# A hybrid attention layer on one core: 40 narrow columns of the input projection go with the second block

## The chip, the core and the metric

The kernel runs on one core of one Trainium2 chip. The metric is the device time of one execution in microseconds (us), as the median over several executions. The matrix engine is called TensorE or PE, and its weight loads PEld; VectorE is DVE, ScalarE is ACT, GpSimd is POOL, SyncE is SP. SP issues nearly all loads.

## The reference

One decoder layer for 256 rows of width 2048, all in float32. What matters here is the combined input projection: one product with `w_in` (2048 x 5672), whose columns feed both groups of heads.

```python
GLA_HEADS, GLA_GATE_RANK, NSA_HEADS = 4, 16, 8
PROJ_SIZES = (GLA_QKV, GLA_GATE_RANK, GLA_VW, NSA_QW, NSA_KVW, NSA_KVW, NSA_KVW, NSA_KVW, NSA_KVW, NSA_KVW, 3 * NSA_HEADS)

n = rms_norm(x, attn_norm_g)
proj = n @ w_in
offsets = np.cumsum(PROJ_SIZES)[:-1].tolist()
(g_qkv, g_lr, g_out, nq, kc, vc, ks, vs, kw, vw, ng) = jnp.split(proj, offsets, axis=-1)
...
log_a = jax.nn.log_sigmoid((gate_lr @ gate_w2 + gate_b).astype(jnp.float32)) / GLA_GATE_TAU
o = rms_norm(o, norm_g) * jax.nn.silu(out_gate.astype(jnp.float32)).reshape(b_, s, h, GLA_DV)
...
gates = jax.nn.sigmoid(gate_logits.astype(jnp.float32)).reshape(b_, s, hk, g, 3).transpose(0, 2, 3, 1, 4)
return gb[..., 0:1] * o_cmp + gb[..., 1:2] * o_sel + gb[..., 2:3] * o_win
...
h = x + jnp.concatenate([gla_out, nsa_out], axis=-1) @ w_out
m = rms_norm(h, ffn_norm_g)
return h + (jax.nn.silu(m @ w_gate) * (m @ w_up)) @ w_down
```

Two pieces of the projection are narrow: `g_lr`, the 16 low rank columns that make the decay of the linear attention, and `ng`, the 24 columns that gate the three branches of the sparse attention. The other columns come in 11 pieces of 512: the output gate (2), q and k and v of the linear attention (4), the compressed, selected and window keys with their values (3), and the sparse queries (2).

## The kernel before, in words

**Blocks, chunks, steps.** The projection runs as 11 blocks (`proj`, L297), driven in a fixed order by the `drive` calls at L1376 to L1388. The order is: both halves of the output gate, four blocks for the linear attention, the compressed block (`C_KC`), the selected block (`C_KS`), the window-key block (`C_KW`), two query blocks. A block has four chunks of 512 rows of `w_in`; in the texts chunks are counted through from 0, so that block 2 has chunks 4 to 7 and the window-key block 32 to 35. For each chunk the weights are loaded by one DMA of 1 MB from SP (`load`, L135), into one of three buffers `raw`. `split` (L138) cuts them into two float32r parts, two of the four row tiles at a time: ScalarE copies `raw` to `hi` (L144), VectorE subtracts and writes `lo` (L145). `chunk` (L278) then issues 24 products (L289) for each piece of at most 512 columns: four row tiles `k`, two halves `t` of the 256 rows, three products each (hi by hi, hi by lo, lo by hi). I call one (k, t) with its three products a step; so a chunk has 8 steps.

**Narrow columns.** A bank of the accumulator memory holds 512 columns. Block 1 loads 16 + 512 columns from `C_LR` on, as the low rank columns lie directly ahead of the output gate; so it works in two pieces of 256 and 272 columns and issues two products where a 512-wide block issues one. In the same way the window-key block loads 512 + 24 columns, in pieces of 256 and 280. At its end, `ev_go(0)` (L384) scales the 16 columns and puts `gla_gate` (L438) on the list `later`, and `ev_kv(1)` (L706) makes the sigmoid of the 24.

**The first block** has loads of its own (L184 to L192), cut finer, and takes its weights from `first_chunk` (L353), in turn with the transposes of `x` (L213).

**Side work.** `drive` (L105) lets the block's products yield units; for so many units `side` takes one step of a task from `urgent` or `later`: transposes, the decay passes of the linear attention (L565 to L572 on VectorE, for two heads and seven levels), its score products (L598 on TensorE), key normalisation (L735 to L753 on VectorE). A third list, `background`, is stepped by a counter: `sum_rows` (L1089) loads a pair of row tiles of the feed-forward weights `w_gate` and `w_up` (1 MB in two loads from SP, L1096), adds them on VectorE (L1101, four adds) and writes the sums back from GpSimd's queue (L1105).

**Order.** Each engine runs its own queue in order. A scheduler settles the order from the program's order and from the `issue_after` hints (`behind`). So a `lo` on VectorE can stand behind an add that waits for its load, and a load on SP behind one that waits for a buffer.

## Time and profile before

| | |
|---|---|
| median of three runs | 1101.02 us (1100.81 to 1101.49) |
| span of the profiled execution | 1099.1 us |
| around the span | 1.9 us |
| TensorE busy | 1094.3 us, 100% |
| VectorE busy | 996.3 us, 91% |
| ScalarE busy | 744.5 us, 68% |
| first block begins (TensorE) | 6.1 us |
| first product with `lo` in block 2 | 34.1 us |
| first product with `lo` in the window-key block | 200.8 us |
| one 512-wide chunk without side work | 5.44 us |

How to read it: a timeline row has the start in us, the time that it spans, engine, line, operation, output and inputs, how often it ran in a row (x2), and in brackets the idle time ahead of it and what ended it. Products overlap on TensorE, so the distance between their starts counts and not the duration. A row of groups ends with busy time, the mean of one in ns and the idle time before. In the queue rows of the DMA view stand packets, MB and the time that the packets took, as a share of 16 engines over the window.

### The profile page before, as it was taken

What the parts mean: (1) busy time and instruction counts of PE and PEld (TensorE: products, weight loads), DVE (VectorE), ACT (ScalarE), POOL (GpSimd) and SP (SyncE); (2) the same over time, 40 slices, a digit from 0 to 9 for tenths busy, and PEclk for the clock granted to TensorE, in tenths of its full rate; (3) what the DMA queues carried; (4) which work ended last, traced back from release to release, by engine and by line L of the source; (5) the groups of instructions that cost most, each with busy time, mean ns of one, the idle gap of its engine ahead of it and who ended that gap; (6) DMA issues with size and microseconds to landing.
All of it is one profiled execution on the core that took longest, in us unless ns stands there. A gap on an engine that the chain in (4) does not pass through costs nothing.

```text
span 1099.1 us, 14686 instructions
## 1 busy us (share of the span) xinstructions
PE 1094.3 (100%) x5294; PEld 900.8 (82%) x5294; DVE 996.3 (91%) x1289; ACT 744.5 (68%) x1014; POOL 81.1 (7%) x150
## 2 busy tenths in 40 slices
PE   9999999999999999999999999999999999999998
PEld 8888888987777887888888888888888888888887
DVE  6578879987799988997999999999999999999998
ACT  7645567555675587667585867768585877768685
POOL 4110001033100100000000000000000000000000
PEclk9999999999999999999999999999999999999999
DMA  7999978468886946785566657576665768677663
GB/s 271 340 338 369 394 259 284 167 243 290 307 280 246 331 159 244 234 317 190 182 230 209 211 197 253 184 248 209 213 230 202 251 214 294 208 259 232 235 231 115
DMA packets 128818, 271.15 MB, mean 247 GB/s; under 512 B 7093, under 2 KB 9177, under 8 KB 128746
## 3 DMA queue, kind: packets, MB, share of 16 engines
q1 hardware_dynamic: 115466, 223.61, 59.2%
q0 software_dynamic: 12672, 46.14, 11.3%
q8 instruction: 41, 0.67, 0.2%
q10 hardware_dynamic: 608, 0.47, 0.1%
q14 instruction: 31, 0.25, 0.1%
HBM read 247.12 MB, written 23.07 MB: 246 GB/s over the span
## 4 chain that ended last, share of the span: by engine, by line
PE 89%; DVE 3%; DMA 3%; issue 2%; ACT 2%; POOL 0%; SPq 0%; DVEq 0%; ACTq 0%; POOLq 0%
PE bank L289 41%; PE bank L1169 39%; PE bank L213 3%; DMA g<-in_w_up_dram 2%; PE bank L1310 2%; DVE lo L145 2%; PE bank L967 1%; PE bank L893 1%; DMA raw<-in_w_out_dram 1%; DVE g L1101 1%; ACT hi L144 1%; PE bank L598 0%; PE bank L800 0%; PE bank L203 0%; ACT g L559 0%
## 5 line engine op out<-in xcount | busy, mean ns | idle before, releaser
L1169 PE MATMUL bank<-ftwo,g 128*128 128x512 f32 x1842 | 430.7, 393 | 0.2 <-ACT ftwo L656 0.2
L1169 PEld LDWEIGHTS bank<-ftwo,g 128*128 128x128 f32 x1842 | 341.2, 188 | 77.0 <-DVE ftwo L657 4.0
L289 PE MATMUL bank<-hi,g 128*128 128x512 f32 (+1 forms) x1088 | 322.7, 377 | 0.0
L657 DVE TENSOR_TENSOR ftwo<-fraw,ftwo 128x1536 fp32r<-128x1536 f32 (+1 forms) x130 | 256.8, 1976 | 7.7 <-ACT ftwo L656 6.6
L656 ACT ACTIVATE ftwo<-fraw 128x1536 fp32r<-128x1536 f32 (+1 forms) x130 | 216.0, 1663 | 28.9 <-DMA fraw<-in_w_up_dram 19.1
L289 PE MATMUL bank<-ftwo,g 128*128 128x512 f32 x960 | 220.7, 390 | 0.0
L289 PEld LDWEIGHTS bank<-hi,g 128*128 128x128 f32 x1088 | 191.9, 189 | 30.3 <-issue 1.0
L289 PEld LDWEIGHTS bank<-ftwo,g 128*128 128x128 f32 x960 | 179.7, 188 | 38.3 <-ACT bank L1281 0.3
L144 ACT ACTIVATE hi<-raw 128x1024 fp32r<-128x1024 f32 (+3 forms) x124 | 130.4, 1058 | 94.7 <-PE bank L289 67.1
L289 PE MATMUL bank<-lo,g 128*128 128x512 f32 (+3 forms) x544 | 193.3, 376 | 0.4 <-DVE lo L145 0.3
L145 DVE TENSOR_TENSOR lo<-raw,hi 128x1024 fp32r<-128x1024 f32 (+3 forms) x124 | 149.8, 1217 | 29.6 <-ACT hi L144 29.3
L656 ACT ACTIVATE ftwo<-g 128x1024 fp32r<-128x1024 f32 x76 | 80.4, 1057 | 73.2 <-DVE g L1200 49.9
L289 PEld LDWEIGHTS bank<-lo,g 128*128 128x128 f32 x544 | 98.2, 189 | 15.2 <-DVE lo L145 1.0
L657 DVE TENSOR_TENSOR ftwo<-g,ftwo 128x1024 fp32r<-128x1024 f32 x76 | 92.8, 1221 | 10.3 <-ACT ftwo L656 10.3
L657 DVE TENSOR_TENSOR ftwo<-fsum,ftwo 128x1024 fp32r<-128x1024 f32 x76 | 92.7, 1220 | 1.0 <-ACT ftwo L656 1.0
L656 ACT ACTIVATE ftwo<-fsum 128x1024 fp32r<-128x1024 f32 x76 | 79.6, 1048 | 5.5 <-DVE fsum L1202 3.9
L1293 ACT COPY g<-bank 128x512 f32<-128x512 f32 x80 | 45.9, 588 | 38.6 <-PE bank L289 36.9
L1200 DVE TENSOR_TENSOR g<-fraw 128x1024 f32<-128x1024 f32 x54 | 65.3, 1220 | 0.3 <-DMA fraw<-in_w_up_dram 0.3
L1281 ACT COPY bank<-g 128x512 f32<-128x512 f32 x80 | 45.3, 594 | 14.7 <-DVE f L1230 8.4
L1158 POOL DMA_DIRECT2D g<-sums x20 | 10.6, 531 | 502.1 <-DVE ftwo L657 473.6
L656 ACT ACTIVATE g<-bank 128x512 fp32r<-128x512 f32 x46 | 26.9, 597 | 29.7 <-PE bank L213 21.2
L213 PE MATMUL bank<-ident,g 128*128 128x128 f32 (+3 forms) x230 | 42.9, 277 | 0.1
(249 smaller groups left out, 913.2 us busy)
## 6 DMA issues: line engine op xcount, KB each, us to landing
fraw<-in_w_gate_dram SPq DMA_DIRECT2D x86, 512.0 KB, 4.0
fraw<-in_w_down_dram SPq DMA_DIRECT2D x42, 1024.0 KB, 5.0
raw<-in_w_in_dram SPq DMA_DIRECT2D x36, 1024.0 KB, 7.8
fraw<-in_w_up_dram SPq DMA_DIRECT2D x66, 512.0 KB, 4.8
sums<-g POOLq DMA_DIRECT2D x40, 512.0 KB, 6.5
raw<-in_w_out_dram SPq DMA_DIRECT2D x16, 1024.0 KB, 7.3
g<-in_w_gate_dram SPq DMA_DIRECT2D x20, 512.0 KB, 7.5
g<-in_w_up_dram SPq DMA_DIRECT2D x20, 512.0 KB, 7.8
```

The source lines that it names most:

```text
L144: act(h[:, i:i + n], r[:, k + i:k + i + n], AF.Copy)
L145: last["d"] = TT(o[:, i:i + n], r[:, k + i:k + i + n], f32(h[:, i:i + n]), ALU.subtract)
L213: return nc.tensor.transpose(o, i, ident[:n, :n])
L289: last["mm"] = mm(bk[t], a[:, k, t * P:(t + 1) * P], ws[k][m][:, off:off + w], start=(first_ and k == 0 and i == 0), stop=(end and k == 3 ...
L656: act(hi, ps, AF.Copy)
L657: last["d"] = TT(lo, ps, f32(hi), ALU.subtract)
L893: mm(sv, a[:, j], b, start=(i == 0), stop=False, skip_group_check=True)
L1169: mm(banks[q], x, m, start=todo[q] == total[q], stop=todo[q] == 1)
L1200: TT(s1, r[:, 1:3], r[:, 3:4].to_broadcast([P, 2, 512]), ALU.add)
L1281: last["seed", n] = nc.scalar.copy(banks[qs[n][t]], h_sb[n][:, t, :])
L1293: nc.scalar.copy(h_sb[n][:, t, :], bs[t])
L1310: mm(bk, u, m, start=(first and i == 0), stop=(end and i == 2), skip_group_check=onto)
```

## The change

Block 1 becomes the first half of the output gate alone, 512 columns in one piece. Block 2 takes 16 low rank columns, 512 of the output gate and 24 branch columns, 552 in all, in pieces of 256 and 296. Since these columns don't lie side by side in `w_in`, each of its four chunks is loaded by three DMAs (`fetch_parts`) into one `raw` buffer, which is 552 wide now. The window-key block becomes 512 wide, in one piece. The evacuation of the narrow columns moves along: `gla_gate` is put on `later` at the end of block 2 and no longer of block 1, and the sigmoid of the 24 columns is made there too, and no longer at the end of the window-key block.

```diff
-            t = wp.tile([P, 4 * 536], dt, tag=tag, bufs=bufs, name=f"{tag}_{n_tiles[0]}")
+            t = wp.tile([P, 4 * 552], dt, tag=tag, bufs=bufs, name=f"{tag}_{n_tiles[0]}")
...
+    def fetch_parts(k0, nk, columns):
+        r, at = weight("raw", nk, sum(n for _, n in columns), 3, F32), 0
+        for c0, n in columns:
+            last["dma"] = nc.sync.dma_start(r[:, :, at:at + n], wi[k0 * P:(k0 + nk) * P, c0:c0 + n].rearrange("(k p) w -> p k w", p=P))
+            at += n
+        return r
...
-    W0 = 528
+    W0 = 512
...
-                ws = split(fetch(wi, 4 * q, 4, c0, w), 4, w)
+                ws = split(fetch_parts(4 * q, 4, c0) if isinstance(c0, tuple) else fetch(wi, 4 * q, 4, c0, w), 4, w)
...
-            if b == 0:
+            if b:
                 lr = small([NT, 16])
...
-                    src = bk[t][:, 16:] if b == 0 and at == 0 else bk[t]
-                    n = src.shape[1]
+                    src = bk[t][:, 16:] if b and at == 0 else bk[t]
+                    n = min(src.shape[1], 512 - at)
+                    src = src[:, :n]
...
-            if b == 0:
+            if b:
                 later.append(gla_gate(lr))
+                gate = st["gate"] = cp.tile([P, NT, 24], F32, name="gate")
+                for t in range(NT):
+                    gt = small([24])
+                    TS(gt, banks[1][t][:, 272:], rx[:, t:t + 1], -1.0, ALU.mult, ALU.mult)
+                    TS(gt, gt, 80.0, None, ALU.min)
+                    act(gt, gt, AF.Exp)
+                    TS(gt, gt, 1.0, None, ALU.add)
+                    nc.vector.reciprocal(gate[:, t, :], gt)
...
-    drive([proj(C_LR, ev_go(0), ((0, 256), (256, 272)), first_chunk)], 2)
+    drive([proj(C_GO, ev_go(0), start=first_chunk)], 2)
...
-    drive([proj(C_GO + 512, ev_go(1)), proj(0, ev_conv(0, to_qk(qq, kk))), proj(512, ev_conv(4, to_qk(kk, qq))),
+    drive([proj(((C_LR, 16), (C_GO + 512, 512), (C_NG, 24)), ev_go(1), ((0, 256), (256, 296))), proj(0, ev_conv(0, to_qk(qq, kk))), proj(512, ev_conv(4, to_qk(kk, qq))),
...
-           proj(C_KW, ev_kv(1), ((0, 256), (256, 280))), proj(C_NQ, ev_nq(0))], 2.5)
+           proj(C_KW, ev_kv(1)), proj(C_NQ, ev_nq(0))], 2.5)
```

The first block's loads begin at `C_GO` in place of `C_LR`, and `ev_kv` loses its lines for the 24 columns.

The scheduler orders the queues anew. The first place is SP's queue behind the small loads (L161), where block 2 begins. Before, from the block's third chunk on (`raw` is a chunk's buffer, `g_79` and `g_80` are the first background pair, `g_97` and `g_98` the second; `raw_732` belongs to block 3):

```order
L135 DMA raw_652<-in_w_in_dram 128x4x512
L135 DMA raw_690<-in_w_in_dram 128x4x512
L1096 DMA g_79_562<-in_w_gate_dram 128x2x512
L1096 DMA g_80_563<-in_w_up_dram 128x2x512
L135 DMA raw_732<-in_w_in_dram 128x4x512
L135 DMA raw_774<-in_w_in_dram 128x4x512
L1096 DMA g_97_669<-in_w_gate_dram 128x2x512
L1096 DMA g_98_670<-in_w_up_dram 128x2x512
```

Now, from the third chunk on (`raw_582`; the fourth is `raw_646`; the pairs are `g_78` with `g_79` and `g_91` with `g_92`):

```order
L152 DMA raw_582<-in_w_in_dram 128x4x16
L152 DMA raw_582<-in_w_in_dram 128x4x512
L1102 DMA g_78_464<-in_w_gate_dram 128x2x512
L1102 DMA g_79_465<-in_w_up_dram 128x2x512
L152 DMA raw_582<-in_w_in_dram 128x4x24
L1102 DMA g_91_608<-in_w_gate_dram 128x2x512
L1102 DMA g_92_609<-in_w_up_dram 128x2x512
L152 DMA raw_646<-in_w_in_dram 128x4x16
L152 DMA raw_646<-in_w_in_dram 128x4x512
L152 DMA raw_646<-in_w_in_dram 128x4x24
L135 DMA raw_732<-in_w_in_dram 128x4x512
```

Both background pairs have moved ahead of the block's fourth chunk, the first pair ahead of the last 24 columns of the third.

The second place is VectorE's queue around the third chunk of the window-key block. Before (`lo_2181` and `lo_2185` are the two halves of that chunk; L753 writes the selected keys; L565 to L572 are decay passes):

```order
L572 TENSOR_TENSOR g_349_2114<-g_349_2114,g_17_134 128x16x16
L145 TENSOR_TENSOR lo_2181<-raw_2178,hi_2180 128x2x536
L753 SCALAR_TENSOR_TENSOR g_320_1977<-bank_2133,kgain,g_319_1976 128x2x128
L753 SCALAR_TENSOR_TENSOR g_320_1977<-bank_2144,kgain,g_319_1976 128x2x128
L565 TENSOR_TENSOR g_82_567<-g_82_567,g_81_566 128x8x32
L569 TENSOR_TENSOR g_352_2159<-g_352_2159,g_16_133 128x8x32
L567 TENSOR_TENSOR g_81_566<-g_81_566 128x8x32
L572 TENSOR_TENSOR g_352_2159<-g_352_2159,g_17_134 128x8x32
L145 TENSOR_TENSOR lo_2185<-raw_2178,hi_2184 128x2x536
```

Now (`lo_2152` and `lo_2156` are the two halves; L759 is the former L753, L582 to L589 the former L565 to L572):

```order
L589 TENSOR_TENSOR g_349_2103<-g_349_2103,g_17_134 128x16x16
L759 SCALAR_TENSOR_TENSOR g_322_1998<-bank_2116,kgain,g_321_1997 128x2x128
L759 SCALAR_TENSOR_TENSOR g_322_1998<-bank_2126,kgain,g_321_1997 128x2x128
L582 TENSOR_TENSOR g_109_748<-g_109_748,g_108_747 128x8x32
L586 TENSOR_TENSOR g_352_2136<-g_352_2136,g_16_133 128x8x32
L584 TENSOR_TENSOR g_108_747<-g_108_747 128x8x32
L589 TENSOR_TENSOR g_352_2136<-g_352_2136,g_17_134 128x8x32
L145 TENSOR_TENSOR lo_2152<-raw_2149,hi_2151 128x2x512
L145 TENSOR_TENSOR lo_2156<-raw_2149,hi_2155 128x2x512
```

The first half's `lo` has moved behind the two key passes and one level of decay, directly ahead of the second half's.

The third place is TensorE's queue at the same chunk. Before, the chunk begins with its products alone (two pieces, so every product stands twice; `bank_2010` to `bank_2013` are the accumulators):

```order
L289 MATMUL bank_2010<-hi_2180,g_45_279 128x256
L289 MATMUL bank_2012<-hi_2180,g_45_279 128x280
L289 MATMUL bank_2010<-lo_2181,g_45_279 128x256
L289 MATMUL bank_2012<-lo_2181,g_45_279 128x280
L289 MATMUL bank_2010<-hi_2180,g_46_280 128x256
L289 MATMUL bank_2012<-hi_2180,g_46_280 128x280
```

Now (L296 is the former L289, L615 the former L598, the score products):

```order
L296 MATMUL bank_2031<-hi_2151,g_43_246 128x512
L296 MATMUL bank_2032<-hi_2151,g_43_246 128x512
L615 MATMUL bank_2193<-g_17_134,g_16_133 128x128
L615 MATMUL bank_2193<-g_16_133,g_17_134 128x128
L615 MATMUL bank_2193<-g_317_1952 128x128
L615 MATMUL bank_2193<-g_320_1987 128x128
L615 MATMUL bank_2207<-g_342_2057 128x128
L615 MATMUL bank_2207<-g_343_2075 128x128
L615 MATMUL bank_2207<-g_349_2103 128x128
L296 MATMUL bank_2031<-lo_2152,g_43_246 128x512
```

Seven score products, which stood one by one between the products of the chunk's second half, now stand in a row ahead of the first product with `lo_2152`.

More of the change, by code (lines that the diff above doesn't have):

```diff
@@ L184 @@
     for i in range(2):
-        nc.sync.dma_start(first[0][:, i], wi[i * P:(i + 1) * P, C_LR:C_LR + W0])
+        nc.sync.dma_start(first[0][:, i], wi[i * P:(i + 1) * P, C_GO:C_GO + W0])
     nc.sync.dma_start(x_sb[0][:, :, 256:512], xv[:, :, 256:512])
-    nc.sync.dma_start(first[0][:, 2:4], wi[2 * P:4 * P, C_LR:C_LR + W0].rearrange("(k p) w -> p k w", p=P))
+    nc.sync.dma_start(first[0][:, 2:4], wi[2 * P:4 * P, C_GO:C_GO + W0].rearrange("(k p) w -> p k w", p=P))
     x_sb.append(load_x(1))
@@ L191 @@
         last["dma"] = nc.sync.dma_start(
-            first[1][:, 2 * c:2 * c + 2], wi[(4 + 2 * c) * P:(6 + 2 * c) * P, C_LR:C_LR + W0].rearrange("(k p) w -> p k w", p=P))
+            first[1][:, 2 * c:2 * c + 2], wi[(4 + 2 * c) * P:(6 + 2 * c) * P, C_GO:C_GO + W0].rearrange("(k p) w -> p k w", p=P))
     x_sb += [load_x(2), load_x(3)]
@@ L362, in first_chunk @@
             return res
-        r = first[q] if q < 2 else fetch(wi, 4 * q, 4, C_LR, W0)
+        r = first[q] if q < 2 else fetch(wi, 4 * q, 4, C_GO, W0)
         turn = flip(x_sb[q], q, ag, hi, lo)
@@ L382 @@
     gout = [g4([NT, 512]) for _ in range(2)]
+    st = {}
     def ev_go(b):
         def f(banks):
-            if b == 0:
+            if b:
                 lr = small([NT, 16])
@@ L689, in gla_mix @@
             yield from gla_out(h, res[h])
-    st = {}
     def ev_kc(banks):
@@ L710, in f @@
                     st[name] = g4(shape, F32R)
-            if br == 1:
-                gate = st["gate"] = cp.tile([P, NT, 24], F32, name="gate")
             for t in range(NT):
-                keys, pv = (banks[0][t][:, :S], banks[0][t][:, S:]) if br == 0 else (banks[0][t], banks[1][t][:, :S])
+                keys, pv = banks[0][t][:, :S], banks[0][t][:, S:]
                 vh = st["vh"][:, br, t, :]
@@ L718, in f @@
                 key_norm(br, t, keys)
-                if br == 1:
-                    gt = small([24])
-                    TS(gt, banks[1][t][:, S:], rx[:, t:t + 1], -1.0, ALU.mult, ALU.mult)
-                    TS(gt, gt, 80.0, None, ALU.min)
-                    act(gt, gt, AF.Exp)
-                    TS(gt, gt, 1.0, None, ALU.add)
-                    nc.vector.reciprocal(gate[:, t, :], gt)
         return f
```

## The prediction, made before the change was timed

> **What bounds the kernel now.** First the page as a whole: the share of each engine, and the chain of work that ended last.
>
> ```profile
> span 1099.1 us, 14686 instructions
> PE 1094.3 (100%) x5294; PEld 900.8 (82%) x5294; DVE 996.3 (91%) x1289; ACT 744.5 (68%) x1014; POOL 81.1 (7%) x150
> PE 89%; DVE 3%; DMA 3%; issue 2%; ACT 2%; POOL 0%; SPq 0%; DVEq 0%; ACTq 0%; POOLq 0%
> ```
>
> TensorE never rests, so time can be won only by giving it less to do, and can be lost only where it waits for VectorE's `lo` or a load. Next the groups of products by shape, of TensorE over the whole span: they say how many instructions the change can remove.
>
> ```profile
> L289 PE MATMUL bank<-hi,g 128*128 128x256 f32 x128 | 36.7, 302 | 0.0
> L289 PE MATMUL bank<-hi,g 128*128 128x280 f32 x64 | 17.6, 290 | 0.0
> L289 PE MATMUL bank<-hi,g 128*128 128x272 f32 x64 | 17.1, 290 | 0.0
> ```
>
> With as many `lo` products again by half, block 1 and the window-key block each issue 192 narrow products where a 512-wide block issues 96. The 290 ns overlap, so they price nothing. I took the price from TensorE's timeline, as the distance between `lo` rows, one per (k, t) step. Here are block 1 (two rows eight steps apart), block 2 (four steps apart) and the window-key block (ten steps apart).
>
> ```profile
> 24.16 0.41 PE L289 MATMUL bank<-lo,g 128*128 128x256 f32 x2
> ...
> 30.02 0.40 PE L289 MATMUL bank<-lo,g 128*128 128x256 f32 x2
> ...
> 34.13 0.39 PE L289 MATMUL bank<-lo,g 128*128 128x512 f32 x1
> ...
> 36.85 0.39 PE L289 MATMUL bank<-lo,g 128*128 128x512 f32 x1
> ...
> 200.79 0.41 PE L289 MATMUL bank<-lo,g 128*128 128x256 f32 x2
> ...
> 208.14 0.41 PE L289 MATMUL bank<-lo,g 128*128 128x256 f32 x2
> ```
>
> A step costs (30.02 - 24.16) / 8 = 0.7325 us at 528 columns, (36.85 - 34.13) / 4 = 0.680 at 512, and (208.14 - 200.79) / 10 = 0.735 at 536. A chunk has 8 steps, a block 4 chunks: 32 steps.
>
> **The products.** Block 1 becomes 512 wide: 32 x (0.7325 - 0.680) = 1.68 us less. The window-key block: 32 x (0.735 - 0.680) = 1.76 less. Block 2 goes from 512 to 552 in two products. No row has that width. The line through 528 and 536 gives 0.740 a step; the rate of the 512-wide step (0.680 / 512 for each column) put on top of 536 gives 0.756. I take the middle, 0.748: 32 x 0.068 = 2.18 more (1.92 to 2.42). Net: -1.26 us (-1.52 to -1.02). The columns are the same; 96 instructions fewer are what is left.
>
> **Block 1 can't give all of its share.** In 24 to 28 us both engines that feed TensorE are as full as it is:
>
> ```profile
> 24.00:28.00 4.00, 4.00 (x35) 4.00 (x34) 3.84 (x6) 3.93 (x9) 0.00 (x0) 1.00 0.85 267
> ```
>
> (TensorE 4.00, VectorE 3.84, ScalarE 3.93.) Their passes shrink only from 528 to 512 columns. I let 0.15 of the 1.68 go (0 to 0.5, an estimate): TensorE comes to block 2 some 1.5 us earlier, at 32.4.
>
> **Block 2's loads.** Each chunk's load becomes three: 512 runs of 64 B, the 1 MB as before, 512 runs of 96 B. No row shows such short runs. The nearest are the last output, from ScalarE's queue (128 runs of 512 B and 16 semaphore packets, in a window of 0.5 us: the DMA row of its 40 slices, then the queue), and the kernel's main queue. The row of 28 to 34 us says how full the engines are there.
>
> ```profile
> DMA  0000000015285959899996949394442201000000
> q10 hardware_dynamic: 144, 0.07, 44.6%
> ...
> q1 hardware_dynamic: 115466, 223.61, 59.2%
> ...
> q1 hardware_dynamic: 1138, 2.25, 100.6%
> ```
>
> The output's packets took 0.446 x 16 x 0.5 / 144 = 24.8 ns at 0.07 MB / 144, about 480 B; the main queue's 0.592 x 16 x 1099.1 / 115466 = 90 ns at 1937 B. The line through both falls to some 7 ns at 80 B. So 1024 short packets over 16 engines cost 64 x 7 to 64 x 25 ns, 0.45 to 1.6 us a chunk, added to a stream that is full already. By the rate alone (128 runs in 26 slices of 12.5 ns, 394 a us) it would be 1024 / 394 = 2.6. I take 1.1 a chunk, near the middle of the durations, because the stream is bounded by busy engines (100.6%) and not by a rate of issue. The Trainium skill, "DMA: Bandwidth & Descriptors", Bandwidth, speaks against the change: a 64 KB load takes 0.95 us there and a 4 KB one 0.68, and below 64 KB time goes to the descriptors. By that, as an estimate, the two short loads (32 and 48 KB) cost 1.4 to 1.9 us a chunk; no run here shows it yet.
>
> Who waits for it? The first chunk, then the last one. ScalarE's and VectorE's rows of block 2's first chunk, and VectorE's first two background adds, which waited for their load:
>
> ```profile
> 29.63 2.01 ACT L144 ACTIVATE hi<-raw 128x1024 fp32r<-128x1024 f32 x2 [1.70 <-DVE rx L376]
> 30.72 2.36 DVE L145 TENSOR_TENSOR lo<-raw,hi 128x1024 fp32r<-128x1024 f32 x2 [1.20 <-ACT hi L144]
> 41.24 0.69 DVE L1101 TENSOR_TENSOR g<-g 128x512 f32<-128x512 f32 x1 [1.31 <-DMA g<-in_w_up_dram]
> 41.97 0.69 DVE L1101 TENSOR_TENSOR g<-g,g 128x512 f32<-128x512 f32 x1
> ```
>
> First chunk: `hi` began at 29.63 and the first `lo` was ready about 2.3 us later (1.09 to the `lo`, and half of 2.36). With up to 1.1 us more it starts at 30.2 to 30.7 and the first `lo` is there at 32.5 to 33.0; TensorE wants it at 32.4 + 0.2. I take a wait of 0.3 us (0 to 0.8).
>
> Last chunk: in SP's order both pairs of background loads now go ahead of it. Before, four chunks and one pair, 5 MB, had landed at 41.2. A second pair is another 1 MB, which at 2.25 MB in 6 us takes 2.8: 44.0 us, plus four times the price of a chunk. Add 2.3 for `hi` and `lo`: 46.3 + 4 x 1.1 = 50.7. TensorE wants it three chunks after 32.7 at 8 x 0.748 = 5.98, with some 0.5 of transposes between: 51.2. No wait; the cover ends at (51.2 - 46.3) / 4 = 1.2 us a chunk, and beyond it each 0.1 costs 0.4. The third chunk's first `lo` stands behind three adds of the first pair: that pair is there at 41.2 - 2.8 plus 2.5 times the price, three adds of 0.7 and a `lo` of 1.2 follow, 41.7, against 32.7 + 2 x 5.98 + 0.3 = 45.0, so its cover ends at 1.3.
>
> **The stall at 71.9 us.** VectorE waited for a background load, and a `lo` was queued behind two adds (VectorE, then TensorE):
>
> ```profile
> 69.32 0.69 DVE L1101 TENSOR_TENSOR g<-g 128x512 f32<-128x512 f32 x1 [5.63 <-DMA g<-in_w_up_dram]
> 70.05 0.69 DVE L1101 TENSOR_TENSOR g<-g,g 128x512 f32<-128x512 f32 x1
> 70.66 1.22 DVE L145 TENSOR_TENSOR lo<-raw,hi 128x1024 fp32r<-128x1024 f32 x1
> ```
>
> ```profile
> 71.03 0.61 PE L289 MATMUL bank<-hi,g 128*128 128x512 f32 x2
> 71.93 0.50 PE L289 MATMUL bank<-lo,g 128*128 128x512 f32 x1 [0.28 <-DVE lo L145]
> ```
>
> The two `hi` rows leave at 71.03 + 2 x 0.227 (0.680 / 3) = 71.48, so TensorE lost 0.45. Afterwards one add stands ahead of that `lo`, not two, the pair's load is the same step behind its chunk, and TensorE comes 0.95 later (-1.53 + 2.18 + 0.3). I give 0.4 back (0 to 0.45); next in line are the following `lo`s, behind the three other adds.
>
> **The window-key block.** VectorE is the bound around its third chunk; its rows, then TensorE's:
>
> ```profile
> 211.93 1.27 DVE L145 TENSOR_TENSOR lo<-raw,hi 128x1072 fp32r<-128x1072 f32 x1
> 213.12 0.87 DVE L753 SCALAR_TENSOR_TENSOR g<-bank,kgain,g 128x256 fp32r<-128x256 f32 x2
> 213.91 0.41 DVE L565 TENSOR_TENSOR g<-g,g 128x256 f32<-128x256 f32 x1
> 214.24 0.42 DVE L569 TENSOR_TENSOR g<-g,g 128x256 f32<-128x256 f32 x1
> 214.57 0.42 DVE L567 TENSOR_TENSOR g<-g 128x256 f32<-128x256 f32 x1
> 214.91 0.42 DVE L572 TENSOR_TENSOR g<-g,g 128x256 f32<-128x256 f32 x1
> 215.25 1.27 DVE L145 TENSOR_TENSOR lo<-raw,hi 128x1072 fp32r<-128x1072 f32 x1
> ```
>
> ```profile
> 213.26 0.51 PE L289 MATMUL bank<-lo,g 128*128 128x256 f32 x2
> ...
> 217.16 0.38 PE L598 MATMUL bank<-g,g 128*128 128x128 f32 x2
> 217.30 0.49 PE L289 MATMUL bank<-hi,g 128*128 128x256 f32 x2
> ...
> 221.09 0.49 PE L289 MATMUL bank<-hi,g 128*128 128x256 f32 x2
> ```
>
> Before, that `lo` was done at 213.1 and TensorE used it at 213.26. Now it stands behind the two L753 (213.12 to 213.91, 0.79 us) and four decay passes (213.91 to 215.25, 1.34): done at 213.1 + 0.79 + 1.34, some 215.25. TensorE alone would want it at 200.79 + 2 x 5.44 + 0.65 of transposes (what 213.26 - 200.79 has over 2 x 5.88), 212.3; seven score products, 0.14 each by the row at 217.16, now stand ahead of it: 213.3. It waits about 1.9 us. Then 22 products at 0.227 and one score product: the fourth chunk starts at 215.25 + 4.99 + 0.14 = 220.4, against 221.09, and saves its own 0.44. The block wins 0.7 + 0.44 = 1.1 of its 1.76; 0.66 is lost (0 to 1.76). The score products that run early are not lost, they were in this chunk before.
>
> The rest (Silu, gate and low-rank passes at another block's end, SP's eight extra issues) lies off TensorE's path.
>
> **The sum.** -1.26 + 0.15 + 0.3 - 0.4 + 0.66 = -0.55. The profiled span of 1099.1 becomes 1098.55; the median, 1101.02, has 1.9 us around it that don't change: **1100.5 us**. What a measurement tells from no change is 0.2%, 2.2 us.
>
> **Rivals.** *All fits:* no wait at block 2 or in the window-key block, and the stall at 71.9 gone: -1.26 - 0.45 = -1.7, 1099.3 us. Against it stand the `lo`'s new place and VectorE's unbroken rows. *It doesn't do what it says:* the window-key block is VectorE's, so narrow or wide products cost the same there (0 of 1.76), while block 2 pays its 2.18: -0.55 + 1.1 = +0.55, 1101.6 us. For it speaks the same full VectorE; against it, that the fourth chunk has no such wait. *Slower:* the short loads bound block 2. Place: TensorE at the first `lo` of chunk 4, behind ScalarE, behind the load. It decides from 1.2 us a chunk; from 1.9 the kernel is over 2.2 us slower (4 x 0.7 = 2.8, less 0.55). At 1.6, the upper end of the durations, it costs 4 x 0.4 = 1.6, less 0.55: 1102.1 us. At the rate of 394 runs a us, 2.6 a chunk: 4 x 1.4 = 5.6, and 0.5 more at the first chunk, less 0.55: 1106.6 us. For it: a stream that is full, 8 more loads, and runs shorter than any priced here. Against it: 25 ns for 512 B. By the Trainium skill's table (the page and section named above) the estimate of 1.4 to 1.9 a chunk would make it 1101.3 to 1103.3 us.
>
> **Chances.** Forecast 0.48, all fits 0.11, no saving 0.11: same 0.70. Slower by over 0.2%: 0.22, all of it the loads. Faster by over 0.2% needs 2.2 us where the whole removed work is 1.5: only by shifts after the change that I don't see, 0.08. The range leaves out these and the upper part of the loads' case, and reaches to 2.2 us a chunk: 1098.9 to 1104.8.
>
> **What would show it.** Right: steps of 0.68 in block 1 and the window-key block and 0.74 to 0.756 in block 2; a TensorE wait under 0.8 us near 32.5; `lo` of the window-key block's third chunk directly behind four decay passes with TensorE idle for 1 to 2.5 us near 213; no stall near 72. Wrong: loads of block 2 that land later than 51 us, short runs over 20 ns each, or a TensorE gap at its third or fourth chunk; or a median outside 1098.8 to 1103.2.

## The result and the profile after

| | before | after |
|---|---|---|
| median (range), first comparison, five runs each | 1100.81 us (1100.24 to 1101.49) | 1106.19 us (1104.91 to 1109.29) |
| ratio, 95% interval | | 1.0052 [1.0041, 1.0063] |
| span of the profiled execution | 1099.1 us | 1103.2 us |
| its own time | 1101.0 us | 1104.91 us |

The change made the kernel 5.4 us slower, outside the range of the prediction (1098.9 to 1104.8) and, at 0.5%, beyond the 0.2% within which it had forecast no difference. The profiled execution of after is the fastest of its five, so its trace explains 4.1 us, not all of the 5.4. The page of after, its span, engines and chain:

```profile
span 1103.2 us, 14510 instructions
PE 1093.5 (99%) x5198; PEld 893.9 (81%) x5198; DVE 996.7 (90%) x1289; ACT 744.0 (67%) x1014; POOL 81.4 (7%) x150
PE 81%; DMA 7%; DVE 5%; issue 3%; ACT 2%; POOL 1%; SPq 1%; DVEq 0%; ACTq 0%; POOLq 0%
```

TensorE has 96 instructions and 0.8 us of work less, and the span is 4.1 us longer: the time went into waiting. The chain says the same, TensorE 81% of it instead of 89. TensorE's waits, first of before, then of after (engine, line, what it waited for: us in total, times, longest us):

```profile
PE bank L289 <- DVE lo L145: 0.3, 1, 0.3
```

```profile
PE bank L296 <- DVE lo L145: 1.2, 2, 0.8
PE bank L220 <- DVE g L674: 0.9, 1, 0.9
PE bank L806 <- DVE bank L798: 0.8, 1, 0.8
PE bank L220 <- ACT g L538: 0.7, 1, 0.7
...
PE bank L220 <- ACT g L908: 0.3, 1, 0.3
```

Before, the only wait of the projection's products on VectorE was the 0.3 at 71.9 us. After, one of the new waits is for block 2's first `lo` (0.8 of the 1.2); most of the others are for side work, in blocks whose columns were not touched: transposes (L220) that wait for the mix of the linear attention (L674), for the Silu behind the filter of v (L538) or for an exponential (L908), and the products of the key compression (L806), which wait for the clearing of their bank (L798).

To see where, I took the start of each chunk's first product from TensorE's timeline in both traces and subtracted:

| start of chunk | before, us | after, us | after less before | what lies between it and the row above |
|---|---|---|---|---|
| 4 (block 2) | 33.90 | 32.41 | -1.49 | -0.31 ahead of block 1's first product, the rest block 1 at 512 columns |
| 10 | 68.54 | 70.59 | +2.05 | block 2: 32 steps at 0.753, and 1.2 at its first chunk |
| 12 | 80.01 | 81.47 | +1.46 | the stall at 71.9 is gone |
| 22 | 137.19 | 138.93 | +1.74 | +0.24 at chunk 12 |
| 23 | 143.32 | 145.81 | +2.49 | transposes wait at 141.4 |
| 32 (window-key) | 200.56 | 203.07 | +2.51 | |
| 36 | 232.19 | 233.66 | +1.47 | window-key block at 512 columns |
| 38 | 248.81 | 251.45 | +2.64 | transposes wait at 247.4 |
| 42 | 275.73 | 279.26 | +3.53 | compression waits at 277.9 |
| 46 | 308.51 | 312.61 | +4.10 | transposes wait at 307 |
| 48 | 326.73 | 331.01 | +4.28 | |
| 59, the last of the output projection | 406.40 | 410.65 | +4.25 | |

Chunks 44 to 59 are those of the output projection (`w_out`). From chunk 48 on nothing more is won or lost in this pair of traces. The places on which the prediction rests come first. TensorE's timeline at block 1 (three steps apart), at block 2's first chunk, over its steps (15 apart), and where the stall had been:

```profile
24.64 0.39 PE L296 MATMUL bank<-lo,g 128*128 128x512 f32 x1
...
26.68 0.39 PE L296 MATMUL bank<-lo,g 128*128 128x512 f32 x1
...
33.75 0.52 PE L296 MATMUL bank<-lo,g 128*128 128x256 f32 x2 [0.82 <-DVE lo L145]
...
39.88 0.42 PE L296 MATMUL bank<-lo,g 128*128 128x256 f32 x2
...
51.18 0.42 PE L296 MATMUL bank<-lo,g 128*128 128x256 f32 x2
...
71.49 0.39 PE L296 MATMUL bank<-lo,g 128*128 128x512 f32 x1
```

Block 1's step is (26.68 - 24.64) / 3 = 0.680, block 2's (51.18 - 39.88) / 15 = 0.753. Block 2's first `lo` came 0.82 us late; at 71.5 the `lo` product has no wait. ScalarE's rows for the first and the last chunk of block 2:

```profile
31.23 2.14 ACT L144 ACTIVATE hi<-raw 128x1104 fp32r<-128x1104 f32 x2 [4.20 <-DMA raw<-in_w_in_dram]
...
46.50 2.14 ACT L144 ACTIVATE hi<-raw 128x1104 fp32r<-128x1104 f32 x2 [4.25 <-DMA raw<-in_w_in_dram]
```

The first chunk began at 31.23 where 29.63 stood before, and now waited for its load. The last was there at 46.5, and TensorE began on it at 51.69, so TensorE waited for no load inside the block. The window-key block, VectorE, then TensorE:

```profile
214.30 0.87 DVE L759 SCALAR_TENSOR_TENSOR g<-bank,kgain,g 128x256 fp32r<-128x256 f32 x2
...
216.43 2.35 DVE L145 TENSOR_TENSOR lo<-raw,hi 128x1024 fp32r<-128x1024 f32 x2
```

```profile
212.18 0.59 PE L220 MATMUL bank<-ident,g 128*128 128x128 f32 x2 [0.28 <-DVE g L747]
...
216.04 1.28 PE L615 MATMUL bank<-g 128*128 128x128 f32 x10
217.69 0.50 PE L296 MATMUL bank<-lo,g 128*128 128x512 f32 x1 [0.37 <-DVE lo L145]
```

The `lo` does stand behind L759 and four decay passes, and TensorE fills most of the time with score products that it would have had later.

Now a stall that nothing in the prediction covers. VectorE around the clearing of the compression's bank (L792, now L798), before:

```profile
269.77 0.67 DVE L1101 TENSOR_TENSOR g<-g,g 128x512 f32<-128x512 f32 x1
...
273.23 0.37 DVE L865 TENSOR_SCALAR sc<-sc,rx 128x4 f32<-128x4 f32 x2 [1.58 <-POOL sc L216]
273.62 0.17 DVE L792 MEMSET bank<- 128x128 f32 x1
```

And after:

```profile
274.98 0.36 DVE L871 TENSOR_SCALAR sc<-sc,rx 128x4 f32<-128x4 f32 x2 [1.54 <-POOL sc L223]
275.25 0.69 DVE L1107 TENSOR_TENSOR g<-g,g 128x512 f32<-128x512 f32 x1
275.85 1.22 DVE L145 TENSOR_TENSOR lo<-raw,hi 128x1024 fp32r<-128x1024 f32 x1
276.99 0.69 DVE L1107 TENSOR_TENSOR g<-g,g 128x512 f32<-128x512 f32 x1
277.70 0.17 DVE L798 MEMSET bank<- 128x128 f32 x1
```

TensorE there, before and after:

```profile
274.38 1.08 PE L800 MATMUL bank<-g,g 128*30 128x128 f32 x32
```

```profile
277.92 1.08 PE L806 MATMUL bank<-g,g 128*30 128x128 f32 x32 [0.82 <-DVE bank L798]
```

Before, the clearing came directly behind the two small operations that wait for GpSimd, and the adds had been done ahead of that wait. After, two adds and a `lo`, 277.70 - 275.25 = 2.45 us, stand between them, and TensorE waits 0.82 for a clearing that takes 0.17. At 247.4 it is the same with another pair. VectorE before (the mix, L657, now L674, came ahead of the `lo`), then VectorE and TensorE after:

```profile
243.80 0.68 DVE L657 TENSOR_TENSOR g<-bank,g 128x512 fp32r<-128x512 f32 x1
...
245.93 1.21 DVE L145 TENSOR_TENSOR lo<-raw,hi 128x1024 fp32r<-128x1024 f32 x1
```

```profile
244.80 1.22 DVE L145 TENSOR_TENSOR lo<-raw,hi 128x1024 fp32r<-128x1024 f32 x1
246.60 0.17 DVE L651 TENSOR_SCALAR sm<-sm 128x2 f32<-128x2 f32 x1 [0.58 <-POOL sm L223]
246.68 0.69 DVE L674 TENSOR_TENSOR g<-bank,g 128x512 fp32r<-128x512 f32 x1
```

```profile
247.42 0.44 PE L220 MATMUL bank<-ident,g 128*128 128x128 f32 x2 [0.95 <-DVE g L674]
```

The mix (L674) stands behind a small operation that waits for GpSimd, with a `lo` ahead of both; its four transposes wait 0.95 us.

### The profile page after: what moved, and what is told of

Its sections match the earlier page's. It is cut to its first block, busy times and chain, and to the rows that moved or that the text cites. A ratio compares the mean times of both kernels' runs of the same rounds, so it can differ in the third digit from the quotient of the medians.

```text
span 1103.2 us, 14510 instructions
## 1 busy us (share of the span) xinstructions
PE 1093.5 (99%) x5198; PEld 893.9 (81%) x5198; DVE 996.7 (90%) x1289; ACT 744.0 (67%) x1014; POOL 81.4 (7%) x150
## 4 chain that ended last, share of the span: by engine, by line
PE 81%; DMA 7%; DVE 5%; issue 3%; ACT 2%; POOL 1%; SPq 1%; DVEq 0%; ACTq 0%; POOLq 0%
PE bank L1175 39%; PE bank L296 35%; DMA g<-in_w_up_dram 3%; PE bank L220 3%; DMA raw<-in_w_in_dram 2%; PE bank L1316 2%; DVE lo L145 2%; PE bank L973 1%; DMA g<-in_x_dram 1%; DMA raw<-in_w_out_dram 1%; ACT hi L144 1%; DVE g L1107 1%; POOL sm L223 1%; POOL sc L223 0%; PE bank L899 0%
## 5 line engine op out<-in xcount | busy, mean ns | idle before, releaser
L296 PE MATMUL bank<-hi,g 128*128 128x512 f32 (+2 forms) x1024 | 321.5, 389 | 0.5 <-ACT hi L347 0.4
L674 DVE TENSOR_TENSOR ftwo<-fraw,ftwo 128x1536 fp32r<-128x1536 f32 (+1 forms) x130 | 256.4, 1974 | 7.4 <-ACT ftwo L673 6.6
L296 PE MATMUL bank<-ftwo,g 128*128 128x512 f32 x960 | 220.5, 390 | 0.0
L296 PEld LDWEIGHTS bank<-hi,g 128*128 128x128 f32 x1024 | 185.0, 188 | 32.8 <-issue 1.0
L296 PEld LDWEIGHTS bank<-ftwo,g 128*128 128x128 f32 x960 | 179.6, 188 | 38.3 <-ACT bank L1287 0.3
L296 PE MATMUL bank<-lo,g 128*128 128x512 f32 (+2 forms) x512 | 193.2, 389 | 1.2 <-DVE lo L145 1.2
L144 ACT ACTIVATE hi<-raw 128x1024 fp32r<-128x1024 f32 (+2 forms) x124 | 130.1, 1058 | 91.5 <-PE bank L296 58.6
L145 DVE TENSOR_TENSOR lo<-raw,hi 128x1024 fp32r<-128x1024 f32 (+2 forms) x124 | 149.7, 1215 | 31.9 <-ACT hi L144 31.5
L296 PEld LDWEIGHTS bank<-lo,g 128*128 128x128 f32 x512 | 94.8, 189 | 17.1 <-DVE lo L145 2.3
L674 DVE TENSOR_TENSOR ftwo<-g,ftwo 128x1024 fp32r<-128x1024 f32 x76 | 92.6, 1218 | 10.6 <-ACT ftwo L673 10.6
L674 DVE TENSOR_TENSOR ftwo<-fsum,ftwo 128x1024 fp32r<-128x1024 f32 x76 | 92.5, 1217 | 0.7 <-ACT ftwo L673 0.5
L673 ACT ACTIVATE g<-bank 128x512 fp32r<-128x512 f32 x46 | 27.0, 598 | 30.7 <-PE bank L220 22.1
L220 PE MATMUL bank<-ident,g 128*128 128x128 f32 (+3 forms) x230 | 42.6, 275 | 2.5 <-DVE g L674 0.9
```

The costliest lines, as they stand in the source:

```text
L144: act(h[:, i:i + n], r[:, k + i:k + i + n], AF.Copy)
L145: last["d"] = TT(o[:, i:i + n], r[:, k + i:k + i + n], f32(h[:, i:i + n]), ALU.subtract)
L220: return nc.tensor.transpose(o, i, ident[:n, :n])
L296: last["mm"] = mm(bk[t], a[:, k, t * P:(t + 1) * P], ws[k][m][:, off:off + w], start=(first_ and k == 0 and i == 0), stop=(end and k == 3 ...
L673: act(hi, ps, AF.Copy)
L674: last["d"] = TT(lo, ps, f32(hi), ALU.subtract)
```

## The experiments

In the expectations, A is the theory that the loss lies in VectorE's and ScalarE's queues, which the scheduler ordered anew far behind the edit; B that the short loads cost it, the prediction's slower rival; V, from the third set of runs on, that background loads landing late hold the adds and what is queued behind them. Each ratio is against the kernel before on the same chip (medians 1102.04, 1101.84, 1102.69 and 1102.32 us in the four sets: runs 1 to 3 with `e_after_again`; `e_pinned`, `e_no_narrow_pinned` and run 6; run 7 and the counter of 6 in run 8; the rest). The sets ran on different chips, so across sets only the ratios are compared.

**1. One load in place of three** (`e_oneload`: after, but block 2 takes 552 columns that lie side by side; the narrow columns hold other values than the reference's).

```diff
-    drive([proj(((C_LR, 16), (C_GO + 512, 512), (C_NG, 24)), ev_go(1), ((0, 256), (256, 296))), ...
+    drive([proj(C_GO + 512 - 16, ev_go(1), ((0, 256), (256, 296))), ...
```

> Changed kernel, but each chunk of block 2 is one load of 552 columns that lie side by side (so its narrow columns hold other columns of w_in): the 8 short loads are gone, the widths and nearly the whole order of VectorE's queue stay those of the changed kernel. Theory A (order: the loss behind block 2, some 3.8 us in the profiled run, comes from lo and background adds that the new order of VectorE's queue puts ahead of steps that TensorE waits for): the first chunk's wait of about 1 us goes, the stalls near 140, 211, 246, 277 and 306 us stay, 1104 to 1105.5 us, 3 to 4.5 over before. Theory B (loads: the short runs make block 2 late, and with it the adds and all that follows): 1100 to 1101.5 us, no stall behind block 2.

Measured: 1106.26 us, 1.0043 [1.0027, 1.006]. TensorE's waits:

```profile
PE bank L220 <- ACT g L538: 3.8, 1, 3.8
...
PE bank L806 <- DVE bank L798: 1.0, 1, 1.0
PE bank L220 <- DVE g L674: 0.9, 1, 0.9
PE bank L296 <- DVE lo L145: 0.8, 2, 0.4
```

A loss stays without the short loads, and so do the stalls at L806, L674 and L538; only the wait for a `lo` is shorter, 0.4 at most. Whether all of the loss stays is less clear: on this chip the changed kernel itself stood at 1.0083 (run 4), 4.3 us above this run. The trace is of the slowest of the seven executions. Its 3.8 is one add on VectorE that waited for its load, with a filter pass and then the transposes behind it:

```profile
141.01 0.69 DVE L1107 TENSOR_TENSOR g<-g 128x512 f32<-128x512 f32 x1 [3.43 <-DMA g<-in_w_up_dram]
```

**2. The short loads alone** (`e_before_short`: before, with the eight short loads into the unused end of wider buffers).

```diff
+    def fetch_more(k0, c0):
+        r = weight("raw", 4, 552, 3, F32)
+        for at, n, c in ((512, 16, C_LR), (0, 512, c0), (528, 24, C_NG)):
+            last["dma"] = nc.sync.dma_start(r[:, :, at:at + n], ...)
+        return r[:, :, :512]
```

> Kernel before, with the 8 short loads of the change added to block 2's chunks (into the same buffer, their columns are never used): VectorE's and ScalarE's queues are those of before but for two or three places, and TensorE's work is that of before. Theory A (order): at most the wait of the first chunk, 1101 to 1102.3 us, no new stall behind block 2. Theory B (loads): 1104 to 1106 us, stalls behind block 2 as in the changed kernel.

Measured: 1102.09 us, 1.0001 [0.9991, 1.0011]. In the order of before the loads cost nothing that can be measured, nor do the wider buffers. A expected no new stall behind block 2, and there is one in the trace: the filter's transposes wait 0.91 us at 140.2, behind an add that waited 2.04 for its load. B, that the short loads as such make the loss, falls here; run 1 alone doesn't exclude a share of them.

**3. The narrow columns left out** (`e_no_narrow`: after, with 11 blocks of 512 columns; the 40 columns are not computed, and other columns stand in for them).

```diff
-    drive([proj(((C_LR, 16), (C_GO + 512, 512), (C_NG, 24)), ev_go(1), ((0, 256), (256, 296))), ...
+    drive([proj(C_GO + 512, ev_go(1)), ...
```

> Changed kernel with the 40 narrow columns left out of the projection (the gates are made of other columns): all 11 blocks are 512 wide, no short loads, 192 products fewer than before, VectorE's queue in nearly the order of the changed kernel. Theory A (order): the changed kernel less 32 steps of 0.073 (2.3 us) less the first wait of 1: 1102 to 1103.5 us, slower than before in spite of 3.4 us less work on TensorE. Theory B (loads): before less 3.4 us, 1097 to 1098 us.

Measured: 1103.63 us, 1.0013 [1.0, 1.0025]. Against before, its products cost 32 x (0.7325 - 0.680) + 32 x (0.735 - 0.680) = 3.4 us less, and it is not faster. The waits are again those of after:

```profile
PE bank L220 <- DVE g L674: 1.0, 1, 1.0
PE bank L220 <- ACT g L538: 0.9, 1, 0.9
PE bank L806 <- DVE bank L798: 0.6, 1, 0.6
```

So some 1.6 (0 to 2.8 by the interval) + 3.4 = 5 us are lost that have nothing to do with narrow columns, short loads or block 2's steps.

**4. The same kernel again** (`e_after_again` and, in the last set, `e_after_third`: after, without an edit).

> The changed kernel once more, for a second profile beside the others on this chip. Theory A (order): 1105 to 1107 us, the stalls at the same steps of the side work (within 0.5 us each). Theory B (loads): the same time, but the stalls move and change in size with how late the loads of block 2 land.

> The changed kernel, for comparison on one chip: 1.005 to 1.0085 of before by both theories.

Measured: 1110.52 us, 1.0083 [1.0053, 1.0112], and 1110.61, 1.0069 [1.0052, 1.0086]. The stalls at L538, L674 and L806 are there in both traces (1.0, 1.1 and 1.6 us in the one, 1.0, 1.0 and 0.8 in the other); the one near 307 is in the second only. Both lose more from 444 to 448 us, where the feed-forward part starts: TensorE waits 2.1 and 1.6 us for VectorE's subtraction (L674), which it does not in the first trace. The subtraction stands behind a `hi` on ScalarE that waits for a load of `w_up`, 3.63 and 2.91 us where it was 0.78 in the first trace. ScalarE in `e_after_again`:

```profile
437.71 1.49 ACT L673 ACTIVATE ftwo<-fraw 128x1536 fp32r<-128x1536 f32 x1 [3.63 <-DMA fraw<-in_w_up_dram]
```

So the size of the loss differs between sets of runs, from 5.4 to 8.5 us, and not only by the stalls above: a load that lands later adds to it.

**5. Hints against three stalls** (`e_pinned`, and again as `e_pinned_again`: in after, the first `lo` of chunk 23 is issued after a filter pass, the second of chunk 38 after the mix, and the first of chunk 42 and the adds after the clearing; `e_no_narrow_pinned`: the same in `e_no_narrow`).

```diff
+    PINS = {23: {0: 'conv_1'}, 38: {1: 'mix'}, 42: {0: 'clear'}}
...
-                last["d"] = TT(o[:, i:i + n], r[:, k + i:k + i + n], f32(h[:, i:i + n]), ALU.subtract)
+                with behind(last.get((first_do or {}).get(k // 2))):
+                    last["d"] = TT(o[:, i:i + n], r[:, k + i:k + i + n], f32(h[:, i:i + n]), ALU.subtract)
...
-            with behind(last["d"]):
+            with behind(last["d"]), behind(last.get("clear")):
```

> Changed kernel with VectorE's queue put back at three places by hints alone: the first lo of chunk 23 goes behind the convolution step that the transposes of v wait for (stall near 140 us), the second lo of chunk 38 behind the pass that frees the transposes' bank (near 246), the background adds and the first lo of chunk 42 behind the clearing of the compression's bank (near 277). Same loads, same products. Theory A (order): those three stalls cost 0.8 to 1.0, 1.2 and 0.9 us in the changed kernel and go; 2 to 3 us faster than the changed kernel, 1102.5 to 1104 us on the scale of the first comparison. Theory B' (the loads and the shift that they bring, whatever the order): within 0.7 us of the changed kernel; the stalls come up elsewhere.

> The kernel without the 40 narrow columns (11 blocks of 512 columns, the gates made of other columns) with the same three hints. Theory A (order): 2 to 3 us faster than the same kernel without hints, which stood at 1.0013 of before; so 0.9985 to 0.9995 of before. Theory B' (an order that can't matter as TensorE waits elsewhere): 1.001 to 1.0015 again.

> The changed kernel with the three hints, on the same chip. Theory A (order): 1 to 2.5 us faster than the changed kernel, with no stall near 277 us and a smaller one near 246. Theory B'' (the stalls in the profile are made up for, or replaced, elsewhere): within 0.7 us of it.

Measured: 1110.01 us, 1.0064 [1.0043, 1.0085]; 1104.56, 1.0024 [1.0007, 1.0041]; 1111.88, 1.0074 [1.0048, 1.01]. All three expectations of a gain missed. In the trace of `e_pinned_again` the hint did at the clearing what it was for (VectorE, TensorE):

```profile
276.10 0.17 DVE L808 MEMSET bank<- 128x128 f32 x1
...
276.22 0.67 DVE L1117 TENSOR_TENSOR g<-g,g 128x512 f32<-128x512 f32 x1
276.81 2.35 DVE L146 TENSOR_TENSOR lo<-raw,hi 128x1024 fp32r<-128x1024 f32 x2
```

```profile
279.10 1.08 PE L816 MATMUL bank<-g,g 128*30 128x128 f32 x32
```

The clearing now stands ahead of the add and the `lo`, and the compression starts without a wait. Of the two other stalls that the hints were aimed at, that of the mix is 0.7 us, where `e_after_third`, the kernel without hints on the same chip, has 1.0; that of the filter grew (second row):

```profile
PE bank L297 <- DVE lo L146: 2.0, 4, 0.8
PE bank L221 <- ACT g L547: 1.5, 2, 1.4
```

The filter's transposes wait 1.5 us in place of 1.0; the waits for a `lo`, 2.0 in place of 2.1, did not change. This execution, the second fastest of its six, is 3.5 us faster than the profiled one of `e_after_third` (1107.04 against 1110.52), but the median is not. That the three stalls make up the median is not shown.

**6. Half of the change each** (`e_lr_only`: after, but the 24 branch columns stay in the window-key block; `e_branch_only`: after, but the 16 low rank columns stay in block 1).

```diff
+    drive([proj(((C_LR, 16), (C_GO + 512, 512)), ev_go(1), ((0, 256), (256, 272))), ...
...
+           proj(C_KW, ev_kv(1), ((0, 256), (256, 280))), proj(C_NQ, ev_nq(0))], 2.5)
```

```diff
+    drive([proj(C_LR, ev_go(0), ((0, 256), (256, 272)), first_chunk)], 2)
...
+    drive([proj(((C_GO + 512, 512), (C_NG, 24)), ev_go(1), ((0, 256), (256, 280))), ...
```

> Half of the change: the 16 low rank columns go with block 2 (528 columns, two loads a chunk), the 24 branch columns stay in the window-key block. By the steps TensorE's work is that of before (-1.68 in block 1, +1.68 in block 2). At the clearing of the compression's bank VectorE's queue stands as in the kernel before, with both adds ahead of the wait for GpSimd. Theory A (order): no stall near 277 us, 0.999 to 1.002 of before. Theory B (loads): half of the loss, 1.002 to 1.003.

> The other half: the 24 branch columns go with block 2 (536 columns, two loads a chunk), the low rank columns stay in block 1. TensorE's work is again that of before (+1.76 in block 2, -1.76 in the window-key block). VectorE's queue stands at the clearing as in the changed kernel, with two adds and a lo between GpSimd's result and the clearing. Theory A (order): a stall of 0.6 to 1.6 us near 277, and 1.002 to 1.004 of before, clearly more than for the other half. Theory B (loads): the same as the other half.

Measured: 1104.14 us, 1.0022 [1.0011, 1.0033], and 1107.57, 1.0055 [1.0035, 1.0074]. Each half is slower by itself. By the number `e_lr_only` lies where B put it (1.002 to 1.003), just outside A's range, though it has no stall at the compression's clearing, as A said; `e_branch_only` lies above both. It has none of the stall at the clearing where A had put one, but waits 2.61 us for one `lo` at 72.9, which stands behind an add that waited 6.40 for its load. So A held as to the kind of loss, not as to its place or size.

**7. Adds that need no load** (`e_after_freeadds`, `e_before_freeadds`: the four adds of a pair work on a scratch tile, so no add waits for a load; what is stored as sums isn't sums, and the scratch tile takes the place of one buffer of the side work).

```diff
-                TT(o, o, i, ALU.add)
+                TT(idle, idle, idle, ALU.add)
```

> Changed kernel in which VectorE's background adds run on a scratch tile in place of the loaded pair (same size, same number; the pairs are still loaded and written back, so the stored sums are not sums): VectorE no longer waits for background loads. (One buffer fewer for the 1024-byte side tiles makes room.) Theory V (a good part of the loss over the profiled run, and the spread of 1104 to 1116 us, is VectorE waiting in turn for a background load that lands late, with a lo or a side step queued behind it): 1 to 3 us faster than the changed kernel, 1.000 to 1.004 of before, the stall near 140 us under 0.4. Theory A alone (places in the queue, whatever the loads): the stalls near 140, 246 and 277 stay, 1.004 to 1.008.

> Kernel before with the same scratch adds. Theory V: 0 to 1 us faster than before (its one stall, 0.45 us at 72, goes, and its runs over 1102 us with it). Theory A alone: within 0.5 us of before. What this and the run before it differ by is what the change costs without any wait for background loads: 0 to 2 us by V, 4 or more by A.

Measured: 1110.47 us, 1.0076 [1.0063, 1.0089], and 1105.47, 1.0028 [1.0017, 1.0038]. Late background loads are out of both kernels, and after is still 5 us behind before: V falls as the cause of the difference. But the stalls did not stay in place, as A alone had it: the one at the clearing is gone, that of the mix is 0.4, and others came. And before itself became 2.8 us slower with less to wait for; its queue was ordered anew too, and its trace has a wait of 2.7 us (L621) that the kernel before doesn't have.

**8. The adds some steps later** (`e_before_late6`, `e_after_late6`, then `e_before_late4`, `e_after_late4`: the counter that separates a pair's loads from its adds runs 6 or 4 steps instead of 3; the projection isn't touched).

```diff
-        for _ in range(3):
+        for _ in range(4):
```

> Kernel before with six steps in place of three. Theory V: equal to before or up to 1 us faster. Theory A alone: an order that was not the one tuned, 1 to 4 us slower than before, as in the changed kernel, though nothing of the projection has changed.

> Changed kernel with six steps of the background counter in place of three between a pair's loads and its adds: the loads have 50 to 70 us more than before to land, and the adds move in VectorE's queue. Theory V: 1 to 3 us faster than the changed kernel. Theory A alone: any order may come out, 1.002 to 1.008 of before, with new stalls at other places.

> Kernel before with four steps in place of three between a background pair's loads and its adds: the same work in another order. Theory A (order: the order before was a good draw, others cost some us): 1 to 4 us slower than before. Theory B'': within 0.7 us.

> Changed kernel with four steps in place of three. Theory A (order): no fixed relation to the changed kernel; against the kernel before with four steps it is 0 to 3 us slower, as the two orders are now alike at the clearing of the compression's bank. Theory B'': 5 us slower than before and than the kernel before with four steps.

| counter | before | after |
|---|---|---|
| 3 | 1102.69 and 1102.32 us | 1110.61 us, 1.0069 [1.0052, 1.0086] |
| 4 | 1108.78, 1.0061 [1.0042, 1.0081] | 1106.24, 1.0035 [1.0023, 1.0046] |
| 6 | 1107.03, 1.0041 [1.0028, 1.0054] | 1109.90, 1.0067 [1.0054, 1.008] |

The kernel before, with one step more and every product, load and add as it was, loses 6.5 us, more than the 1 to 4 that A expected and about as much as the change under study. In its trace, VectorE and TensorE near 118 us:

```profile
115.15 0.69 DVE L1101 TENSOR_TENSOR g<-g 128x512 f32<-128x512 f32 x1 [7.46 <-DMA g<-in_w_up_dram]
...
118.32 1.21 DVE L145 TENSOR_TENSOR lo<-raw,hi 128x1024 fp32r<-128x1024 f32 x1
```

```profile
119.58 0.79 PE L289 MATMUL bank<-lo,g 128*128 128x512 f32 x1 [2.47 <-DVE lo L145]
```

An add that waits 7.46 us for its load stands ahead of a `lo`, and TensorE waits 2.47. (It also waits 3.8 us in four waits for ScalarE, L1065, where the kernel before has none.) The product behind the wait takes 0.79 us, twice the 0.39 of others of its shape, and the granted clock of TensorE is half there. Here is the stretch from 119.6 to 122.9 us of that trace: busy times of PE, PEld, DVE, ACT and POOL, then the granted clock (1.00 in 108 to 117 us and again in 123.2 to 130), the DMA share and GB/s.

```profile
119.60:122.90 3.30, 3.30 (x8) 2.62 (x9) 3.30 (x8) 2.53 (x5) 0.00 (x0) 0.50 0.67 223
```

The half clock lasts some 3.4 us and costs about 1.7 more, an estimate: half of its length. It follows in all four traces with one wait of TensorE of 2.47 us or more (2.47 here, 2.61 in `e_branch_only`, 2.72 in `e_before_freeadds`, 3.85 in `e_oneload`) and, in both traces with a counter of 6, two shorter waits close together near 500 us (1.5 and 0.5, 1.12 and 0.93). In the other traces the clock falls only at the end of the span, when TensorE is done; their longest single wait is 1.65, and the 1.89 that `e_before_late4` has at 413 us is not followed by it either. A mean granted clock of 0.998 or less, which is about what one such stretch makes of 1100 us, stands in none of the 77 runs of the kernel before in these four sets, in 3 of the 10 of the changed kernel (1111.65 us and more, the slowest), and in 5 of the 9 of `e_pinned` (1110.01 us and more; the other four are at 1106.94 or less). So part of the spread, and of some medians, is one long wait and the slow clock behind it.

The changed kernel under the same edit gains 4.4 us and is then the faster of the two by 2.5, where A expected it to be 0 to 3 us slower. With a counter of 6 it stands where it stood with 3. No version tried beats the kernel before.

## Why the prediction was wrong, point by point

**What bounds the kernel: right.** TensorE is busy 99% of a longer span. That time can be lost only by its waiting is what happened.

**The products: right in the price of a step.** The step of block 2 is 0.753 (0.748 taken, 0.740 to 0.756 bounded), 512-wide steps are 0.680. That TensorE reached block 2 at 32.41 (32.4 forecast) is in part luck: 0.31 of the 1.49 us stand ahead of block 1's first product, and in the two other traces of the same kernel block 2 began only 0.43 and 1.11 us earlier than before.

**The price of the short loads: right in size.** The DMA row of after from 28 to 30 us, with packets under 512 B that are the short runs, and the queue's share of 16 engines:

```profile
DMA packets 1232, 0.63 MB, mean 316 GB/s; under 512 B 959, under 2 KB 959, under 8 KB 1232
q1 hardware_dynamic: 1232, 0.63, 112.7%
```

1232 packets took 1.127 x 16 x 2 = 36.1 us. If the 273 long ones took the 90 ns of the prediction's mean, 24.6 us, the 959 short ones took 11.5 / 959 = 12 ns each (the packets' own records in the trace say 11 for 64 B and 12 for 96 B): 64 x 12 = 0.77 us a chunk, inside 0.45 to 1.6 and below the 1.1 taken, so there was no wait at chunks 5 to 7. By the table of the Trainium skill, "DMA: Bandwidth & Descriptors", Bandwidth, the estimate had been 1.4 to 1.9 us a chunk; this trace puts it at about half, and in `e_before_short` eight such loads gave 1.0001 [0.9991, 1.0011].

**The first chunk of block 2: mis-sized.** Forecast 0.3 us (0 to 0.8); chunk 4 lasted 7.23 against 8 x 0.753 = 6.03, so 1.2. The load was there at 31.23, later than the 30.2 to 30.7 of the working, and the first `lo` was ready at 32.39 + 1.31 = 33.7, not 32.5 to 33.0. From the issue of the chunk's first load to `hi` it took 31.23 - 23.74 = 7.5 us here, 31.10 - 24.28 = 6.8 with one load (`e_oneload`) and at most 29.63 - 24.04 = 5.6 before. So some 0.7 of the delay is the short loads'; the larger part is there without them and was not taken apart. That TensorE's wait in `e_oneload` is only 0.38 says less: its first `lo` product came at 33.62, 0.13 earlier than here, and TensorE had reached the block 0.43 later.

**The stall at 71.9: right.** It is gone, and the two chunks there gave 0.59 back (0.4 forecast).

**The window-key block: right in size.** It gave 1.04 of its 1.76 (1.1 forecast). The `lo` stands behind the key passes and four decay passes, as said; the single wait of 1.9 us, which was to be the sign of it, did not come, since the transposes waited first (0.28) and score products filled more of the time, 0.37 being left.

**Where it failed** is one sentence: "The rest (Silu, gate and low-rank passes at another block's end, SP's eight extra issues) lies off TensorE's path." By the terms above the profiled span would be longer by 0.4 us: the forecast -0.55, plus 0.9 for the first chunk and 0.17 for the steps, less 0.19 at the stall, and 0.1 for the two blocks' small differences. The other 3.7 came behind the blocks that I had worked through: 0.24 at chunk 12, 0.75 at 141, 1.17 at 247, 0.89 at 278, 0.57 at 307, 0.18 more by chunk 48, together 3.8, and 0.1 back. None of this is work added: it was put at nothing, and measured 3.7. I looked at the new order at the two places of the edit and took it as unchanged beyond, where it was ordered anew as well, on a VectorE that is 91% busy. At 247 and 278 it is a `lo` and adds that moved ahead of what TensorE needs next.

**The rivals.** The slower rival's upper case gave 1106.6 us, near the 1106.19 measured, and is still wrong: its mechanism (loads that bound block 2) is not in the trace, where each of chunks 5 to 7 takes 6.03 us, eight steps without a wait, and run 2 speaks against it. The chance of 0.22 for slower held the right sign for a false reason; an order that turns out worse had no chance of its own, while 0.08 went to "shifts after the change" on the faster side only. *All fits* and *it doesn't do what it says* both failed by the same omission, and each by a place of its own: the first by the wait at block 2, the second by the 1.04 that the window-key block did give.

**Shown and not shown.** Shown: the short loads alone cost nothing in the order of before (2), and a loss is there without them (1), without the narrow columns' products (3) and without any add that waits for a load (7). The lost time in the profiled run lies in waits for side work whose place in the queue changed, and a new order with nothing else changed moves the time by as much: +6.5 and +4.3 us on the kernel before, -4.4 and nothing clear of the noise on the changed one (8; 1.0067 against 1.0069). Not settled: which of the new places the medians hang on, and how much of them the later load near 437 us and the half clock behind long waits make up. The hints removed one of the three stalls and not the loss (5), and the runs of one changed kernel spread over up to 9 us (1107.23 to 1115.94 in run 4), with losses at other places (near 445 us in run 4) than in the first trace. What share the short loads have once the order is the new one (4.3 us between run 1 and run 4, with intervals that overlap) is open too.

## What to carry to other kernels

Where TensorE is full and VectorE nearly so, a change that saves 0.1 or 0.2% of the products is smaller than what a new order of the queues costs or gives: 0.3 to 0.6% here. Compare the order of the whole program, not only that of the edited place, and give "the order behind it gets worse" a chance and a price of its own, taken from a neutral shift such as one step more in a counter. A rival that hits the number isn't confirmed by it: look whether its wait is in the trace. And read the clock beside a long wait, since the wait's own length may not be all that it costs.

## What the runs showed of the hardware that was not expected

Runs of 64 and 96 B took about 12 ns each on a busy queue (worked out above), about half of the 24.8 ns per packet of the 480 B output. The products of 552 columns in two pieces cost 0.753 us a step where 512 in one cost 0.680, so nothing beyond their columns (0.680 x 552 / 512 = 0.733) but 0.02 us for three more instructions. A single wait of TensorE of 2.47 us or more was followed by 3.4 us at half the granted clock in each of the four traces that have one (run 8). And when a load lands differs between executions of one program: ScalarE waited 0.78, 3.63 and 2.91 us for the same load in the three traces of the changed kernel, and in the last two TensorE waited behind it.
